# Hybrid encoder block on one core: softmax weights, q and k transposed by VectorE in 32x32 blocks and device memory instead of by TensorE

## The chip, the cores and the metric

The kernel runs on one core of a Trainium2 chip. The metric is the device time of one execution in microseconds (us). A core has TensorE (PE: matmuls out of SBUF into PSUM), VectorE (DVE), ScalarE (ACT), GpSimd (POOL) and SyncE (SP). Each works through its own list of instructions in order, and waits at an instruction until what that one needs is there. SP and POOL issue most DMA transfers here. The order of each list is fixed when the program is built.

## The reference

One layer on 512 tokens of width 1024, all float32: a half-step SwiGLU, a mixer, a second half-step SwiGLU. The mixer has a gated linear recurrence and a neighbourhood attention side by side. The part that matters here is the attention:

```python
h = _rmsnorm(x, norm_mix[l])
xr, gr, q, k, v, ga, gb = jnp.split(h @ w_in[l], splits, axis=-1)
...
q = _rmsnorm(q.reshape(B_, S, N_HEADS, HEAD_DIM), q_norm[l]) * (HEAD_DIM ** -0.5)
k = _rmsnorm(k.reshape(B_, S, N_HEADS, HEAD_DIM), k_norm[l])
y_att = _neighbourhood_attention(q, k, v, rel_pos_bias[l])   # 16 heads of 64, softmax over an 8x16 window
y = jax.nn.sigmoid(ga) * y_lru + jax.nn.sigmoid(gb) * y_att
x = x + y @ w_out[l]
```

## The kernel before

**Matmuls and chunks.** A float32 product is made of three fast passes: each operand is split into a high part (ACT copies it to the fast format, `wh`, `xh`) and a low part (DVE subtracts, `wl`, `xl`), and PE does high x high, low x high and high x low (`mm3`, L171 to L174). The weights of the middle stage come in blocks of 512 KB; SP loads a block into `wraw` (three buffers), ACT and DVE split it into `wh` and `wl` (four buffers each), and PE does 24 matmuls of 512 columns on it. Such a block with its 24 matmuls is called a chunk below.

**The order of chunks.** After the eight chunks of the recurrence input (`wxr`) come 24 chunks for q, k and v: heads 0 to 7 (the first half, `hf` 0) get four chunks for q, four for k, four for v, and then heads 8 to 15 (the second half) the same. Then come 24 gate chunks, eight for the GeLU gate, eight for gate A, eight for gate B (L1083 to L1103), and then eight output chunks (`wout`, L1110). Gate B chunk f is multiplied with the attention output `att[f]`, split into `yh`, `yl` and used as k-block f of every output chunk. So the loop over gate B asks for `att[f]` before it goes on: `until("att", ...)` at L1096, with the batches of `GB_BATCH` (f = 0 to 3, then 4 and 5, then 6, then 7).

**Attention is woven in between.** `heads(hf, raws, st)` is a generator. `weave` (L577) calls it a fraction of a step at each chunk (`RATE`: 0.75 steps in stage `t1`, 0.7 steps twice a chunk in stage `g`), and each `yield` ends a step. Both halves stand in one lane, the second behind the first. When `until` finds that `att[f]` isn't there, it runs all the steps that are missing, with no chunk between them.

**One half of the attention.** q and k come out of PE with tokens on the partitions (four tiles of 128 tokens each, `raws`). They are scaled by their norm (L902). `start(fi)` turns one pair of heads: eight PE transposes into PSUM (L911, L913), and from there ACT and DVE write the high and low parts (`qh`, `ql`, `kh`, `kl`). `scores` does the score matmuls (L943), then DVE adds the bias and takes the maximum (L963), ACT the exponential (L970), and DVE scales by the sum (L972, L975). The softmax weights of one block pair `n2` are in two tiles, `inner` (four 128x128 blocks) and `outer` (three). `turn` transposes those seven on PE (L982, L989) and ACT copies them out of PSUM. `apply` multiplies with V (L1006) and ACT writes `att`. A unit of this loop is one `n2` of one head pair in the first half (eight units), and a whole head pair in the second (four units).

**POOL's list.** POOL issues the copies that put the gates of the recurrence on other partitions (L759), the rearrangement of V through device memory (`vd` written at L860, read at L863 and L873), and the bias tiles `bm` (L885).

Of the kernel before, what the change touches and what calls it, by code (L numbers as in the profile page):

```python
# [9 lines left out]
F32 = mybir.dt.float32  # L10
F32R = mybir.dt.float32r
AF = mybir.ActivationFunctionType
ALU = mybir.AluOpType
# [3 lines left out]
P = 128  # L17
# [9 lines left out]
NCB, QC = 4, 16  # L27
# [64 lines left out]
def block_kernel(ctx: ExitStack, tc, a, out):  # L92
# [30 lines left out]
    def aux_t():  # L123
        return aux.tile([P, T], F32, tag="aux", name=nm("aux"))
# [126 lines left out]
    def hold(i):  # L251

        after(i, mark["mm"])
        return i
# [426 lines left out]
    gk = small[:, C_KN : C_KN + 1]  # L681

    state = {}

    def perm(ap):

        return ap.rearrange("p (r j c) -> p j r c", r=ROWS, j=NCB)
# [200 lines left out]

    def heads(hf, raws, st):

        rq = tiny.tile([P, 2, NCB, 8], F32, tag="rq", name=nm("rq"))
        for w in range(2):
            for j in range(NCB):
# [5 lines left out]
        for w in range(2):  # L899
            for j in range(NCB):  # L900
                t = raws[w][j].rearrange("p (h d) -> p h d", d=HD)
                hold(nc.vector.tensor_tensor(t, t, rq[:, w, j, :].unsqueeze(2).to_broadcast([P, 8, HD]), ALU.mult))  # L902
            yield
        qk, rss, soft, PTs = {}, {}, {}, {}


        def start(fi):
            fs = slice(fi * P, (fi + 1) * P)
            pq, pk = aux_t(), aux_t()
            for j in range(NCB):  # L910
                hold(nc.tensor.transpose(pq[:, j * P : (j + 1) * P], raws[0][j][:, fs], ident))  # L911
            for j in range(NCB):
                hold(nc.tensor.transpose(perm(pk)[:, j], raws[1][j][:, fs], ident))  # L913
            rev = lambda t: t.rearrange("p (j t) -> p j t", j=NCB)[:, :, ::-1]
            fwd = lambda t: t.rearrange("p (j t) -> p j t", j=NCB)
            qh, ql, kh, kl = (big_t(F32R, n=n) for n in ("qh", "ql", "kh", "kl"))
            nc.scalar.activation(rev(qh), fwd(pq), AF.Copy, scale=gq8)
            with tc.high_priority():
                nc.vector.scalar_tensor_tensor(rev(ql), fwd(pq), gq8, rev(qh.bitcast(F32)), ALU.mult, ALU.subtract)
            nc.scalar.activation(kh, pk, AF.Copy, scale=gk)  # L920
            with tc.high_priority():
                mark["kl"] = nc.vector.scalar_tensor_tensor(kl, pk, gk, kh.bitcast(F32), ALU.mult, ALU.subtract)
            grid = lambda t: t.rearrange("p (r c) -> p r c", r=ROWS)
            qk[fi] = qh, ql, grid(kh), grid(kl)

        def scores(fi, n2s):

# [47 lines left out]
                    nc.vector.tensor_scalar(pt, pt, rs[:, hp, n : n + 1], None, ALU.mult)  # L975
            return mm

        def turn(fi, n2):
            outer, inner = soft.pop((fi, n2))
            pT = aux_t()  # L980
            for q in range(4):
                hold(nc.tensor.transpose(pT[:, q * P : (q + 1) * P], inner[:, q * P : (q + 1) * P], ident))  # L982
            PTi = big_t(n="PT")
            with tc.high_priority():
                nc.scalar.activation(PTi, pT, AF.Copy)

            pT = aux_t()
            for q in range(3):
                hold(nc.tensor.transpose(pT[:, q * P : (q + 1) * P], outer[:, q * P : (q + 1) * P], ident))  # L989
            PTe = big_t(n="PT")  # L990
            with tc.high_priority():
                nc.scalar.activation(PTe[:, : 3 * P], pT[:, : 3 * P], AF.Copy)
            PTs[fi, n2] = PTe, PTi

        def apply(fi, behind=None):
            pv = aux_t()
            for n in range(NCB):
                PTe, PTi = PTs[fi, n // 2]
                for half in range(2):
                    if n in EDGE:  # L1000
                        vt = V[hf, "single" if half else "own", n]
                    else:
                        vt = V[hf, (KSTART[n] + half * QC) // 8]
                    for h2 in range(2):
                        q = (1 if half else h2 * 2) if n in EDGE else h2 * 2 + half
                        mm = nc.tensor.matmul(  # L1006
                            pv[h2 * HD : (h2 + 1) * HD, n * P : (n + 1) * P],
                            vt[:, (fi * 2 + h2) * HD : (fi * 2 + h2 + 1) * HD],
                            (PTe if n in EDGE else PTi)[:, q * P : (q + 1) * P],
                            start=half == 0, stop=half == 1)  # L1010
# [16 lines left out]
        def turns(i, k=0):  # L1027

            if not 0 <= i - LB < len(units):
                return False  # L1030
            fi, n2s = units[i - LB]
            turn(fi, n2s[k])
            return k + 1 < len(n2s)

        for i in range(len(units) + LC):
            together = phase[0] != "g"
            if together:
                turns(i)
            if i < len(units):
                fi, n2s = units[i]  # L1040
                last = scores(fi, n2s)
                if i >= LC and 1 in units[i - LC][1]:
                    apply(units[i - LC][0], last)
# [5 lines left out]
            if not together:  # L1049
                yield  # L1050
                if turns(i):
                    yield
                    turns(i, 1)
            if len(units) <= i < len(units) + LC and 1 in units[i - LC][1]:
                apply(units[i - LC][0])
            yield

    att = [None] * KT
    phase = ["t0"]
# [153 lines left out]
```

## Time and profile before

The median of three runs is 1116.77 us. The profiled execution spans 1114.8 us from its first to its last instruction.

| what | value |
|---|---|
| median of 3 runs | 1116.77 us (1116.19 to 1116.80) |
| profiled execution, span | 1114.8 us |
| idle time ahead of PE's groups | 1.1 us, all before the first matmul |
| DMA over the span | 161.16 MB, 145 GB/s |
| POOL queue / SP queue share of the DMA engines | 19.0% / 32.9% |

How to read the views: the page's first part has the busy time of each engine, its second the span in 40 slices, its fourth the chain of work that ended last. The groups of instructions give the line, the engine, the operation, output and inputs, the count, the busy time of the group, the mean duration of one in ns, and the idle time ahead of them. The timeline gives start and length of instructions in order of time, with equal neighbours merged (xN).

### The profile page before, as it was taken

To read this page: it belongs to the slowest core of one execution; us is meant where nothing else is said; L and a number is where in the kernel's file an instruction comes from. 1 tells how busy PE (TensorE), PEld (TensorE's weight loads), DVE (VectorE), ACT (ScalarE), POOL (GpSimd) and SP (SyncE) were. 2 spreads that over 40 slices of the span, in tenths; PEclk is the share of its full clock that TensorE was granted. 3 is DMA by queue.
4 is the path that set the end of the run, shared out by engine and by line. 5 is a ranking of instruction groups with operands and counts; after the bars stand their busy time and mean duration, and the time that the engine had idled before them with its cause. 6 is when DMAs were issued, how large, how long until landed. Compare 5 with 4: busy or idle time off the path is not lost.

```text
span 1114.8 us, 17726 instructions
## 1 busy us (share of the span) xinstructions
PE 1110.2 (100%) x6923; PEld 985.2 (88%) x6923; DVE 797.4 (72%) x1263; ACT 592.2 (53%) x903; POOL 109.8 (10%) x187
## 2 busy tenths in 40 slices
PE   9999999999999999999999999999999999999998
PEld 8899999988888778788888888888999999998887
DVE  7877777794745776999665976659877777784542
ACT  8554554563533678877364554346645444563330
POOL 0000000000000351250140000001000000000000
PEclk9999999999999999999999999999999999999999
DMA  8566656743423585673453332277766666652421
GB/s 266 154 168 152 156 154 164 166 137 95 137 84 111 165 249 153 178 195 100 137 162 100 99 100 74 77 246 156 198 148 163 153 168 145 160 170 96 132 76 38
DMA packets 54116, 161.16 MB, mean 145 GB/s; under 512 B 8464, under 2 KB 12048, under 8 KB 54032
## 3 DMA queue, kind: packets, MB, share of 16 engines
q1 hardware_dynamic: 39744, 118.31, 32.9%
q0 software_dynamic: 13712, 41.46, 19.0%
q8 instruction: 54, 0.88, 0.3%
q10 hardware_dynamic: 576, 0.26, 0.1%
q14 instruction: 30, 0.25, 0.1%
HBM read 143.19 MB, written 8.39 MB: 136 GB/s over the span
## 4 chain that ended last, share of the span: by engine, by line
PE 100%; DVE 0%; issue 0%
PE acc L312 31%; PE acc L172 11%; PE acc L173 10%; PE acc L174 10%; PE aux L312 5%; PE acc L831 4%; PE acc L832 4%; PE acc L833 4%; PE aux L172 4%; PE aux L173 4%; PE aux L174 4%; PE aux L1006 1%; PE aux L742 1%; PE aux L943 1%; PE aux L982 1%; PE acc L464 1%
## 5 line engine op out<-in xcount | busy, mean ns | idle before, releaser
L145 ACT ACTIVATE wh<-wraw 128x1024 fp32r<-128x1024 f32 (+3 forms) x224 | 220.7, 988 | 318.8 <-issue 93.4
L148 DVE TENSOR_TENSOR wl<-wraw,wh 128x1024 fp32r<-128x1024 f32 (+3 forms) x236 | 267.4, 1137 | 123.7 <-ACT wh L145 122.5
L312 PE MATMUL acc<-s,wh 128*128 128x256 f32 x1280 | 232.3, 283 | 0.0
L312 PEld LDWEIGHTS acc<-s,wh 128*128 128x128 f32 x1280 | 199.6, 192 | 0.1
L312 PE MATMUL acc<-s,wl 128*128 128x256 f32 x640 | 181.1, 283 | 0.0
L312 PEld LDWEIGHTS acc<-s,wl 128*128 128x128 f32 x640 | 122.9, 192 | 0.0
L172 PE MATMUL acc<-xh,wh 128*128 128x512 f32 x272 | 108.4, 398 | 0.0
L174 PE MATMUL acc<-xh,wl 128*128 128x512 f32 x272 | 106.6, 392 | 0.0
L173 PE MATMUL acc<-xl,wh 128*128 128x512 f32 x272 | 106.3, 391 | 0.0
L312 PE MATMUL acc<-xh,wl 128*128 128x256 f32 x320 | 90.6, 283 | 0.0
L312 PE MATMUL acc<-xl,wh 128*128 128x256 f32 x320 | 90.6, 283 | 0.0
L312 PE MATMUL acc<-xh,wh 128*128 128x256 f32 x320 | 90.5, 283 | 0.0
L831 PE MATMUL acc<-wh,xh 128*128 128x512 f32 x192 | 75.7, 394 | 0.0
L832 PE MATMUL acc<-wh,xl 128*128 128x512 f32 x192 | 74.8, 389 | 0.0
L833 PE MATMUL acc<-wl,xh 128*128 128x512 f32 x192 | 74.7, 389 | 0.0
L172 PE MATMUL aux<-hh,wh 128*128 128x512 f32 (+1 forms) x181 | 69.9, 386 | 0.0
L173 PE MATMUL aux<-hl,wh 128*128 128x512 f32 (+1 forms) x181 | 69.9, 386 | 0.0
L174 PE MATMUL aux<-hh,wl 128*128 128x512 f32 (+1 forms) x181 | 69.9, 386 | 0.0
L174 PE MATMUL acc<-hh,wl 128*128 128x512 f32 (+1 forms) x176 | 67.9, 386 | 0.0
L173 PE MATMUL acc<-hl,wh 128*128 128x512 f32 (+1 forms) x176 | 67.9, 386 | 0.0
L172 PE MATMUL acc<-hh,wh 128*128 128x512 f32 (+1 forms) x176 | 67.9, 386 | 0.0
L148 DVE TENSOR_TENSOR wl<-pair,wh 128x1024 fp32r<-128x1024 f32 x40 | 48.9, 1222 | 20.9 <-ACT wh L145 20.9
(225 smaller groups left out, 2288.9 us busy)
## 6 DMA issues: line engine op xcount, KB each, us to landing
wraw<-wqkv SPq DMA_DIRECT2D x24, 512.0 KB, 5.0
wraw<-wg SPq DMA_DIRECT2D x24, 512.0 KB, 3.6
wraw<-w1d SPq DMA_DIRECT2D x22, 512.0 KB, 3.6
wraw<-w2s SPq DMA_DIRECT2D x22, 512.0 KB, 4.1
pair<-w2s SPq DMA_DIRECT2D x22, 512.0 KB, 5.2
wraw<-w2d SPq DMA_DIRECT2D x22, 512.0 KB, 3.7
wraw<-w1s SPq DMA_DIRECT2D x18, 512.0 KB, 4.1
pair<-w1s SPq DMA_DIRECT2D x18, 512.0 KB, 5.5
```

The source lines that it names most:

```text
L145: nc.scalar.activation(H, raw, AF.Copy)
L148: return nc.vector.tensor_tensor(L, raw, H.bitcast(F32), ALU.subtract)
L172: nc.tensor.matmul(ps, wh, xh, start=first, stop=False, skip_group_check=skip)
L173: nc.tensor.matmul(ps, wh, xl, start=False, stop=False, skip_group_check=skip)
L174: mark["mm"] = nc.tensor.matmul(ps, wl, xh, start=False, stop=last, skip_group_check=skip)
L312: mm = nc.tensor.matmul(o, w_[:, c], x_, start=first and m + k == 0 and w_ is H and x_ is xh_, stop=m + k == 4 and w_ is L, skip_group_che ...
L464: nc.tensor.matmul(pre[i], w[i][1][:, s], xh[k], start=k == 0, stop=False)
L742: prev, mm = mm, nc.tensor.matmul(ps[d][b], W[w][o, c], X[x][o], start=x == 1, stop=w + x == 0)
L831: nc.tensor.matmul(pss[j], xh[kk][:, tj], H[:, s], start=kk == 0, stop=False)
L832: nc.tensor.matmul(pss[j], xl[kk][:, tj], H[:, s], start=False, stop=False)
L833: mark["mm"] = nc.tensor.matmul(pss[j], xh[kk][:, tj], L[:, s], start=False, stop=kk == KT - 1)
L943: mm = hold(nc.tensor.matmul(ps[hp][:, cs], q_[o, n * P : (n + 1) * P], keys(k_[o]), start=k_ is kl, stop=q_ is ql))
```

## The change

Nothing is transposed by PE in the attention any more. DVE has a transpose of 32x32 blocks; the blocks are then put in their places by a write to device memory and a read back.

- q and k: behind each scaling of a token tile, DVE transposes its blocks into `qkt`, and POOL writes it to `qd` in four DMAs: 8 tiles, 32 DMAs for each half. `fetch(g)` reads two head pairs of q and k back on SP, 512 KB each, into `xqk` (two buffers). `start` then reads `xqk` in place of PSUM. The norm weights of k are folded into q's.
- softmax weights: `ship` replaces `turn`. DVE transposes the blocks of `outer` and `inner` into `pt` (one buffer), POOL writes `pt` to `pd` (one DMA), and reads it back into `PT` (three buffers) in four DMAs, once for each unit and `n2`: 16 times.
- the steps: two more `yield`s and `fetch(0)` before the first `start`; in stage `g` each turn of the loop has three steps in both halves, and `ATT_LAG` is one number. `NBIG` goes from 48 to 43.

```diff
-ATT_LAG = (1, 2), (1, 2)
+ATT_LAG = 2, 2
...
-    NBIG = 48
+    NBIG = 43
...
                 hold(nc.vector.tensor_tensor(t, t, rq[:, w, j, :].unsqueeze(2).to_broadcast([P, 8, HD]), ALU.mult))
+                t2 = big_t(n="qkt")
+                nc.vector.transpose(
+                    t2.rearrange("p (c f i) -> p f c i", c=NCB, i=32), raws[w][j].rearrange("p (f c i) -> p f c i", c=NCB, i=32))
+                for ab in range(NCB):
+                    nc.gpsimd.dma_start(
+                        qd[w].rearrange("(c i) j a x -> j a i c x", c=NCB)[j, ab],
+                        t2[ab * 32 : (ab + 1) * 32].rearrange("p (c x) -> p c x", c=NCB))
             yield
+
+        def fetch(g):
+            for w in range(2):
+                x = big.tile([P, 16, 2, 32], F32, tag="xqk", bufs=2, name=nm("xqk"))
+                nc.sync.dma_start(
+                    x.rearrange("p x f i -> p x (f i)"), qd[w].rearrange("p j a (g x) -> g p (j a) x", g=2)[g])
+                for f in range(2):
+                    xs[w, g * 2 + f] = x[:, :, f]
+
+        yield
+        fetch(0)
+        yield
...
         def start(fi):
-            for j in range(NCB):
-                hold(nc.tensor.transpose(pq[:, j * P : (j + 1) * P], raws[0][j][:, fs], ident))
-            for j in range(NCB):
-                hold(nc.tensor.transpose(perm(pk)[:, j], raws[1][j][:, fs], ident))
...
+            if fi == 1:
+                fetch(1)
...
-        def turn(fi, n2):
+        def ship(fi, n2):
+
             outer, inner = soft.pop((fi, n2))
...
+            t = big.tile([P, NCB, 7, 32], F32, tag="pt", bufs=1, name=nm("pt"))
...
+            nc.vector.transpose(to[:, 4:], sub(outer, 3))
+            nc.vector.transpose(to[:, :4], sub(inner, 4))
+            d = dram.tile([P, NCB, 7 * 32], F32, tag="pd", bufs=4, name=nm("pd"))
+            nc.gpsimd.dma_start(d, t.rearrange("p c q i -> p c (q i)"))
+            PT = big.tile([P, NCB, 7, 32], F32, tag="PT", bufs=3, name=nm("PT"))
+            for j in range(4):
+                q = slice(j * 32, (j + 1) * 32)
+                nc.gpsimd.dma_start(PT[:, j].rearrange("p q i -> p (q i)"), d[q].rearrange("i c x -> c i x"))
...
-        LB, LC = ATT_LAG[hf]
+        LC = ATT_LAG[hf]
...
         for i in range(len(units) + LC):
...
+                behind = scores(fi, n2s)
+            if i >= LC and 1 in units[i - LC][1]:
+                apply(units[i - LC][0], behind)
+            if i < len(units):
+                for n2 in n2s:
+                    ship(fi, n2)
...
+            yield
+            if phase[0] == "g":
                 yield
-                if turns(i):
-                    yield
-                    turns(i, 1)
...
+                yield
```

The rows below are from the lists of the built programs: line, operation, output<-inputs, shape. The line numbers are each program's own; in the changed one the scores stand at L962, `apply` at L1024, the `qd` writes at L909, `fetch` at L917, the `pd` write and `PT` reads at L1006 and L1010.

PE before, at the first unit of the second half (the last two score matmuls, then the transposes for the next head pair, then a gate A chunk; the eleventh of the 24 gate chunks stands ahead of the score matmuls):

```order
L943 MATMUL acc_6391<-kh_6368,ql_6367 128x256
L943 MATMUL acc_6390<-kh_6368,ql_6367 128x256
L911 MATMUL aux_6456<-ident,qk_5090 128x128
L911 MATMUL aux_6456<-ident,qk_5092 128x128
L911 MATMUL aux_6456<-ident,qk_5094 128x128
L911 MATMUL aux_6456<-ident,qk_5096 128x128
L913 MATMUL aux_6457<-ident,qk_5323 128x8x16
L913 MATMUL aux_6457<-ident,qk_5325 128x8x16
L913 MATMUL aux_6457<-ident,qk_5327 128x8x16
L913 MATMUL aux_6457<-ident,qk_5329 128x8x16
L172 MATMUL acc_6478<-xh_3088,wh_6480 128x512
```

PE after, at the same first unit of the second half, which now stands behind the chunk of gate B f=5, the 22nd of the 24:

```order
L172 MATMUL acc_6789<-xh_3102,wh_6791 128x512
L173 MATMUL acc_6789<-xl_3103,wh_6791 128x512
L174 MATMUL acc_6789<-xh_3102,wl_6792 128x512
L962 MATMUL aux_6810<-kl_6784,qh_6781 128x256
L962 MATMUL aux_6809<-kl_6784,qh_6781 128x256
L962 MATMUL aux_6810<-kh_6783,qh_6781 128x256
```

And PE after, from the end of that unit's 24 score matmuls to the next unit's:

```order
L962 MATMUL acc_6812<-kh_6783,ql_6782 128x256
L962 MATMUL acc_6811<-kh_6783,ql_6782 128x256
L962 MATMUL aux_6929<-kl_6900,qh_6897 128x256
L962 MATMUL aux_6928<-kl_6900,qh_6897 128x256
L962 MATMUL aux_6929<-kh_6899,qh_6897 128x256
```

The second half's scores moved behind 22 gate chunks, where eleven stood ahead of them before, and there is no chunk between the first and the second unit. From there PE's list reads: scores of units 0, 1 and 2, `apply` of unit 0, scores of unit 3, `apply` of unit 1, the chunk of gate B f=6, half of `apply` of unit 2, 14 matmuls of the chunk of f=7, the other half of unit 2, the rest of f=7 and 13 matmuls of output chunk 0, half of `apply` of unit 3, 19 more matmuls of output chunks 0 and 1, and the other half of unit 3.

POOL before, where V of the second half is rearranged in the stage of the first half's attention (`vd` is the device memory copy, `va` and `ve` the edge tiles):

```order
L863 DMA vs_5666<-vd_82 128x1x512
L869 MEMSET ve_5669 128x512
L873 DMA va_5668<-vd_82 64x4x64 x2
L873 DMA ve_5669<-vd_82 64x4x64
L873 DMA va_5668<-vd_82 64x4x64 x2
L873 DMA ve_5669<-vd_82 64x4x64
L869 MEMSET ve_5678 128x512
L873 DMA va_5677<-vd_82 64x4x64 x2
L873 DMA ve_5678<-vd_82 64x4x64
L873 DMA va_5677<-vd_82 64x4x64 x2
L873 DMA ve_5678<-vd_82 64x4x64
L885 DMA bm_5942<-rpb 128x640
```

POOL after, from the end of that same rearrangement:

```order
L873 DMA va_5587<-vd_82 64x4x64 x2
L873 DMA ve_5588<-vd_82 64x4x64
L885 DMA bm_5651<-rpb 128x640
L885 DMA bm_5930<-rpb 128x640
L885 DMA bm_5932<-rpb 128x640
L1006 DMA pd_5634<-pt_5631 128x896
L1010 DMA PT_5636<-pd_5634 128x1x224 x4
L1006 DMA pd_5794<-pt_5791 128x896
L1010 DMA PT_5796<-pd_5794 128x1x224 x4
```

The round trips of the first half's units 2 and 3 stand behind the rearrangement of V; before, nothing of the attention but bias tiles stood behind it.

POOL after, at the second half (the last two of the eight groups of q and k writes, and the first round trips):

```order
L909 DMA qd_6573<-qkt_6673 32x4x128 x4
L909 DMA qd_6573<-qkt_6680 32x4x128 x4
L885 DMA bm_7024<-rpb 128x640
L885 DMA bm_7026<-rpb 128x640
L1006 DMA pd_6880<-pt_6877 128x896
L1010 DMA PT_6882<-pd_6880 128x1x224 x4
L885 DMA bm_7144<-rpb 128x640
L1006 DMA pd_6890<-pt_6887 128x896
L885 DMA bm_7146<-rpb 128x640
L1010 DMA PT_6892<-pd_6890 128x1x224 x4
L1006 DMA pd_6999<-pt_6996 128x896
L1010 DMA PT_7001<-pd_6999 128x1x224 x4
```

The four reads of each round trip stand right behind its write, and the next write behind them; eight such groups follow each other for the second half. Before, POOL had only the bias tiles there.

More of the change, by code (lines that the diff above doesn't have):

```diff
@@ L680, in block_kernel @@
     nc.vector.tensor_scalar(gq8, small[:, C_QN : C_QN + 1], HD**-0.5, None, ALU.mult)
-    gk = small[:, C_KN : C_KN + 1]
+    nc.vector.tensor_tensor(gq8, gq8, small[:, C_KN : C_KN + 1], ALU.mult)
     state = {}
@@ L889, in heads @@
     def heads(hf, raws, st):
+        xs = {}
+        qd = [dram.tile([P, NCB, NCB, P], F32, tag="qd", bufs=4, name=nm("qd")) for _ in range(2)]
         rq = tiny.tile([P, 2, NCB, 8], F32, tag="rq", name=nm("rq"))
@@ L909, in start @@
[L909 to L915 removed]
+            xq, xk = (xs[w, fi].rearrange("p (j a) i -> p j a i", j=NCB) for w in range(2))
@@ L997, in apply @@
             for n in range(NCB):
-                PTe, PTi = PTs[fi, n // 2]
+                PT = PTs[fi, n // 2]
                 for half in range(2):
@@ L1024, in heads @@
         yield
-        LB, LC = ATT_LAG[hf]
[L1027 to L1033, printed above, removed]
+        LC = ATT_LAG[hf]
         for i in range(len(units) + LC):
-            together = phase[0] != "g"
-            if together:
-                turns(i)
+            behind = None
             if i < len(units):
                 fi, n2s = units[i]
-                last = scores(fi, n2s)
-                if i >= LC and 1 in units[i - LC][1]:
-                    apply(units[i - LC][0], last)
+                behind = scores(fi, n2s)
[4 more added lines that the diff above has]
+                    ship(fi, n2)
                 if 0 in n2s:
```

36 lines of the change are left out of this document (12 added, 24 removed).

## The prediction

> **What bounds the kernel now.** First the page's busy times, then the span in slices, then the chain.
>
> ```profile
> span 1114.8 us, 17726 instructions
> PE 1110.2 (100%) x6923; PEld 985.2 (88%) x6923; DVE 797.4 (72%) x1263; ACT 592.2 (53%) x903; POOL 109.8 (10%) x187
> PE   9999999999999999999999999999999999999998
> PE 100%; DVE 0%; issue 0%
> ```
>
> PE is busy in every slice, and the chain that ended last is PE alone. So PE's list is the time: what leaves it counts in full, and so does each new wait in it. No other engine matters until it makes PE wait. The span and the median of 1116.77 us lie 2.0 us apart; I work against the span and add the 2.0 at the end.
>
> **What is removed.** Here are transposes among matmuls in PE's timeline (start, length), then the two groups of the softmax weights and the two of q and k.
>
> ```profile
> 651.75 0.39 PE L174 MATMUL acc<-xh,wl 128*128 128x512 f32 x1
> 651.98 0.60 PE L982 MATMUL aux<-ident,p 128*128 128x128 f32 x4
> 652.41 0.49 PE L989 MATMUL aux<-ident,p 128*128 128x128 f32 x3
> 652.66 0.48 PE L172 MATMUL acc<-xh,wh 128*128 128x512 f32 x1
> 652.98 0.40 PE L173 MATMUL acc<-xl,wh 128*128 128x512 f32 x1
> L982 PE MATMUL aux<-ident,p 128*128 128x128 f32 x64 | 9.6, 272 | 0.0
> L989 PE MATMUL aux<-ident,p 128*128 128x128 f32 x48 | 7.9, 273 | 0.0
> L911 PE MATMUL aux<-ident,qk 128*128 128x128 f32 x32 | 5.1, 281 | 0.0
> L913 PE MATMUL aux<-ident,qk 128*128 128x128 f32 x32 | 5.0, 273 | 0.0
> ```
>
> The groups' busy sums make 27.6, but neighbours overlap. Without the seven transposes L172 and L173 would start 0.23 and 0.46 after 651.75, at 651.98 and 652.21; L173 starts at 652.98, so seven cost 0.77, or 0.11 each. 64 + 48 + 32 + 32 = 176 of them by 0.11 give **R = -19.4**. All transposes of the attention are gone from PE's new list.
>
> **What the order does to the second half.** Its scores now stand behind 22 gate chunks, 11 later than before, and hardly any work is left to PE while eight softmax round trips run. This is the largest term. Prices: a chunk by PE's pitch, then a unit of the second half (scores, `apply`, and the DVE operation that ends its softmax and the next head's `kl`).
>
> ```profile
> 654.12 0.39 PE L172 MATMUL acc<-xh,wh 128*128 128x512 f32 x1
> 655.25 0.39 PE L174 MATMUL acc<-xh,wl 128*128 128x512 f32 x1
> 655.57 0.39 PE L943 MATMUL aux<-kl,qh 64*128 64x256 f32 x2
> 657.25 0.44 PE L1006 MATMUL aux<-PT,va 128*64 128x128 f32 x4
> 659.14 0.66 PE L911 MATMUL aux<-ident,qk 128*128 128x128 f32 x4
> 662.86 0.74 DVE L922 SCALAR_TENSOR_TENSOR kl<-aux,small,kh 128x512 fp32r<-128x512 f32 x1
> ```
>
> Five matmuls in 1.13 are 0.227 each, so a chunk of 24 is 5.4. Scores take 657.25 - 655.57 = 1.7, `apply` 1.9, and a unit on DVE from the first score to the end of `kl` 663.60 - 655.57 = 8.0.
>
> For POOL: the times of an issue, and of a write to device memory until the read that waits for it (the `vd` rows are the only round trip of this sort in the trace, the bracket has the wait).
>
> ```profile
> 476.23 0.60 POOL L860 DMA_DIRECT2D vd<-v  x1 [0.65 <-DVE v L856]
> 477.48 0.60 POOL L860 DMA_DIRECT2D vd<-v  x1 [0.66 <-DVE v L856]
> 481.85 0.59 POOL L863 DMA_DIRECT2D vs<-vd  x1 [0.78 <-DMA vd<-v]
> 484.97 0.59 POOL L863 DMA_DIRECT2D vs<-vd  x1 [2.52 <-DMA vd<-v]
> 552.72 0.91 POOL L860 DMA_DIRECT2D vd<-v  x1 [0.62 <-DVE v L856]
> 557.23 0.60 POOL L863 DMA_DIRECT2D vs<-vd  x1 [3.59 <-DMA vd<-v]
> L885 POOL DMA_DIRECT2D bm<-rpb x16 | 8.8, 552 | 111.2 <-DVE rs L972 54.0 <-DVE nmx L963 52.4 <-DMA gate<-pair 4.0
> L873 POOL DMA_DIRECT2D va<-vd x16 | 12.4, 776 | 9.5 <-issue 9.3
> bm<-rpb POOLq DMA_DIRECT2D x16, 320.0 KB, 4.2
> xd<-pair SPq DMA_DIRECT2D x16, 256.0 KB, 2.6
> va<-vd POOLq DMA_DIRECT2D x16, 64.0 KB, 3.5
> wraw<-wqkv SPq DMA_DIRECT2D x24, 512.0 KB, 5.0
> 494.99 3.69 DVE L902 TENSOR_TENSOR qk<-qk,rq 128x512 f32<-128x512 f32 x6
> ```
>
> From write to read 481.85 - 476.23 = 5.6 and 484.97 - 477.48 = 7.5. The `vd` write of 552.72 is the last of its kind and its reader starts 4.5 later. I take 5.2 for `pd`, between 4.5 and 5.6; 7.5 is the high end, and the low one 3.2, by SP's writes to device memory, which land in 2.6 behind an issue of 0.6. An issue is 0.55 for 128 rows (`bm`) and 0.78 for 256 (`va`): 0.55 for `pd` and `PT`, 0.65 for the smaller pieces of `qd`.
>
> The reads stand behind the wait for their own write, and the next write behind them. So a ship holds POOL for 5.2 + 4 x 0.55 = **7.4**, and nothing overlaps with the next one.
>
> Set t = 0 where PE ends gate B f=3. Until t = 10.9 PE has the chunks f=4 and f=5. DVE's list puts the eight q and k transposes from behind gate B f=1's product (ready at t = -10.9, then a weight split and two scalings) to just ahead of f=4's (t = 5.4): the first at about -6.6, the last at 5.7.
> - POOL: 32 `qd` writes by 0.65 from -6.6 end at 14.2; the last lands 3.5 later, 17.7; SP's fetch in 256-byte pieces, 5.0 by the `wqkv` row, 22.7; ACT and DVE split, 2 x 0.75 with handoffs, and the scores of the first unit start at **24.7**. PE has waited since 10.9.
> - The first `pt` is ready 8.0 + 1.2 (its two transposes) after: 34. Eight ships by 7.4 are 59, two bias issues stand between, and POOL is through at 94.3. The last read lands after 4 (between 4.2 and 3.5): 98.3. `apply` of that half, the copy, two DVE operations and the split of `y` take 4 more: 102.3, and only then can PE go on with the output chunks.
> - In that time PE has the chunks of gate B f=4 and f=5, four scores, four `apply`, the chunks f=6 and f=7, and 44 matmuls of the first output chunks that need no `att[7]` (32 ahead of the last half of `apply`, 12 behind it): 10.9 + 6.8 + 7.6 + 10.9 + 44 x 0.227 = 46.2.
>
> So **C = 102.3 - 46.2 = +56**. With 5.4 for a ship (3.2 + 2.2) it is 40, and with 9.7 (7.5 + 2.2) it is 74; the `qd` issues at 0.55 take 3 off and at 0.78 add 4, and dear transposes (below) add 5: 37 to 83.
>
> The cost of DVE's block transpose is in no row. The cheap end is an operation on half the elements, 0.42; the nearest row, L902 above on the same elements, makes six in 3.69, 0.6 each, which I take. A recurrence on the same shape is the dear end, 1.2.
>
> ```profile
> L963 DVE CUSTOM_DVE_ANT_0 so<-aux,bm 128x256 f32<-128x256 f32 x24 | 10.1, 419 | 0.0
> L784 DVE TENSOR_TENSOR_SCAN th<-gate,gate 128x512 f32<-128x512 f32 x4 | 4.9, 1216 | 0.0
> ```
>
> At 1.2 the last `qkt` and the first unit are later by about 5 in sum, at 0.42 earlier by 1. The Trainium skill, "VectorE: DVE Perf Modes", section "The three transpose paths", gives 311 ns for 128x128 in bf16 and, under "Rules for kernel authors", advises TensorE for 128x128 where PSUM can take the result; it speaks against this change. By its figure an estimate for 128x512 is 1.24 us, near the dear end, and the sum would be 1173. No run before shows the operation.
>
> **The first half.** Its units are woven between chunks, so that PE waits only for what is late.
>
> ```profile
> 508.51 0.40 PE L833 MATMUL acc<-wl,xh 128*128 128x512 f32 x1
> 501.22 0.78 POOL L873 DMA_DIRECT2D ve<-vd  x1
> 563.83 0.54 POOL L869 MEMSET ve<- 128x512 f32 x1
> 578.49 0.77 POOL L873 DMA_DIRECT2D ve<-vd  x1 [0.24 <-issue]
> ```
>
> Before, the q and k transposes follow 508.51; now `yield`s put four chunks there, so the first scores are asked for at 508.7 + 21.8 = 530.5. POOL is free of V's first rearrangement at 502.0; 32 writes by 0.65 end at 522.8, landing 526.3, fetch 531.3, split 533: **A = +3** (0 where the issues take 0.55, 9 with issues of 0.78 and a landing of 5).
>
> Its ships meet V's second rearrangement on POOL, whose edge tiles alone run from 563.83 to 579.26. Counted through PE's new list from 533 by the prices above, PE wants the weights of units 0 and 1 at 561 (24 scores a unit pair, two chunks and a half between) and those of units 2 and 3 at 585. POOL's list has the first two ships ahead of the edge tiles and the next two behind them. Before 563.83 POOL stood waiting for V's landings, so that I let unit 1's weights land at 565, 4 late. Units 2 and 3 follow at 579.3: 579.3 + 2 x 7.4 + 4 = 598 stands against 585 + 4, 9 late, of which I take 8 since PE's earlier waits count only once: **B = 4 + 8 = +12**, from 0 (ships of 5.4 and two chunks more of cover) to 18 (ships of 9.7).
>
> Hidden: ACT's copies of PSUM go (ACT idles half its time), the folded norm weight, `NBIG` and one bias tile earlier or later. SP waits at `fetch` with weight loads behind it, but its loads run some seven chunks ahead (three raw and four split buffers), and that covers a wait of up to 20 (four chunks).
>
> **Sum:** -19.4 + 3 + 12 + 56 = +51.6; 1114.8 + 51.6 + 2.0 = **1168**.
>
> **Rivals.**
> 1. *Faster: the ships are short enough to be covered*, and R alone is left: 1116.8 - 19.4 = 1097. The point from which it turns: even with A = B = 0, C has to be under 19.4, so that eight ships take 37 less than 59, 2.8 each, when their four reads alone take 2.2 to issue and the shortest write in a row above needs 3.2. For it: only that the trace of before has no ship. Chance 0.03, and 0.02 that it ends within 0.2%.
> 2. *DVE is the bound and not POOL*, since two ships fit into a unit: 4.6 each. Then DVE's 8.0 + 1.2 a unit sets the pace: 24.7 + 4 x 9.2 + 7.4 + 8 = 77, C = 31, the time 1143. Against it: a ship of 4.6 leaves 2.4 from write to read, under the 3.2 of the low end. For it: the rows of `vd` queue behind other writes, which `pd` doesn't. Chance 0.12.
> 3. *PE runs slower after its waits.* In the first row of matmuls after PE's only idle time
>
> ```profile
> L138 PE MATMUL aux<-ones 128*128 128x128 f32 x16 | 3.8, 431 | 1.1 <-DVE pol L667 1.1
> ```
>
>    16 of 128x128 took 3.8, 0.24 each against 0.11 for those above. If each long wait of the drain (14 ahead of the first unit, then about six of 5 to 10) costs that once more, half of 2 to 4 us of work each time is lost, +8: 1176. The Trainium skill, "TensorE: Matmul & The Clock Gate", section "HAM oscillation — how this bites in real kernels", states that rule: after some 3.4 us idle the clock halves until PE has been busy for a while. That row agrees for the start; no row shows it within the kernel. Chance 0.23.
> 4. *The edit isn't what it says*, and transposes stay on PE: PE's list excludes it, under 0.01.
>
> **How the numbers follow.** The forecast's own case has 0.59: 1168, with its own range of 1152 to 1186 by the ends of a ship. Rival 2 (0.12) gives 1143 and rival 3 (0.23) 1176. The lowest sum of all low ends is 1114.8 - 19.4 + 0 + 0 + 37 + 2 = 1134, the highest 1114.8 - 19.4 + 9 + 18 + 83 + 2 + 8 = 1215; not all ends come together, so the range of 8 in 10 runs from 1140 to 1200. A measurement here tells 0.2%, or 2.2 us, from no change. Faster 0.03, same 0.02, slower 0.95.
>
> **What will show it.** Right: PE's idle time 60 to 80 us in one place late in the mixer, with POOL's `PT` and `pd` issues 7.4 apart eight times over, releaser the landing of `pd`; the first scores of the second half wait about 14 for `kh`; PE's busy sum falls by 27.6 while the gaps grow; the chain names POOL and DMA. Wrong in R: a neighbour pitch other than 0.227 where transposes went. Wrong in C: ship periods far from 7.4, or PE working in the gaps. Wrong in A or B: waits ahead of L962 or `apply` in the first half other than 3 and 12. The clock rival: matmul pitches near 0.45, or a granted clock under 1.00, behind gaps.

## The result and the profile after

| | before | after |
|---|---|---|
| median | 1116.78 us (1116.19 to 1117.07) | 1211.65 us (1208.93 to 1212.47) |
| span of the profiled execution | 1114.8 us | 1209.7 us |
| mean granted TensorE clock over the span | 1.000 | 0.953 |

The change made the kernel slower: ratio 1.0845 (95% interval 1.083 to 1.0861), 94.9 us. The sign was forecast; the predicted 1168 lies 43 us under the measured time, and the range ended at 1200.

The page of the changed kernel: span, busy times, the slices of PE and of its granted clock (the share of TensorE's full clock that it was given, in tenths), and the chain.

```profile
span 1209.7 us, 17700 instructions
PE 1112.6 (92%) x6747; PEld 983.2 (81%) x6747; DVE 823.9 (68%) x1312; ACT 582.4 (48%) x874; POOL 197.6 (16%) x331
PE   9999999999999999897869962468999999999998
PEclk9999999999999999899879985588999999999999
PE 32%; issue 1%; DMA 0%; POOL 0%; DVE 0%
```

PE has gaps in two places, slices 17 to 21 (the first half's attention) and 24 to 28 (the second half's), and in the same slices the granted clock falls. PE's busy time has not fallen by the 27.6 of the removed groups: it grew by 2.4. The chain could be followed back only to the last `pd`, 33% of the span in sum, so the sign that it would name POOL and DMA is not decided by it.

What PE waited for (total, times, longest):

```profile
PE aux L1024 <- DMA PT<-pd: 58.4, 10, 11.6
PE aux L962 <- DVE kl L939: 27.9, 4, 11.1
PE acc L831 <- ACT qk L843: 4.9, 1, 4.9
PE aux L1024 <- issue: 1.3, 1, 1.3
```

That is 92.5 of new waits. The bill, all from the two profiled executions: +92.5 of waits; -18.5 for the 176 transposes (the sum of their start-to-start times in the trace of before); and the rest to 94.9 is +20.9, which is time in which the same matmuls ran slower. By place, 27.7 of the waits lie in the first half's stage (4.9 + 11.6 + 0.6 + 10.6) and 64.8 behind gate B f=5.

POOL's timeline through two ships of the second half (start, length, idle time ahead and what ended it):

```profile
745.70 0.58 POOL L1006 DMA_DIRECT2D pd<-pt  x1
746.25 0.56 POOL L885 DMA_DIRECT2D bm<-rpb  x1
751.31 2.04 POOL L1010 DMA_DIRECT2D PT<-pd  x3 [4.50 <-DMA pd<-pt]
755.58 0.66 POOL L1010 DMA_DIRECT2D PT<-pd  x1 [2.23 <-issue]
756.23 0.60 POOL L1006 DMA_DIRECT2D pd<-pt  x1
761.67 2.00 POOL L1010 DMA_DIRECT2D PT<-pd  x3 [4.85 <-issue]
765.96 0.66 POOL L1010 DMA_DIRECT2D PT<-pd  x1 [2.28 <-issue]
766.61 0.60 POOL L1006 DMA_DIRECT2D pd<-pt  x1
```

From one `pd` to the next 756.23 - 745.70 = 10.5, and then 10.4, against 7.4 in the prediction. From write to read it is 5.6 and 5.4, against 5.2 assumed (in the eight ships of the second half 4.9 to 7.3, 5.8 in the mean). The four reads take 4.9 in place of 2.2: 0.67 each, and the fourth doesn't follow the third at once but stands still for 2.2 first. In all eight ships of the second half it starts 0.32 to 0.36 after the landing of the first read (755.22 for the one of 755.58, 765.63 for 765.96). From the first `pd` at 733.71 to the end of the last read's issue at 820.2 the eight ships take 86.5, so 10.8 each.

PE behind a long wait, in the first half:

```profile
580.03 1.12 PE L1024 MATMUL aux<-PT,vs 128*64 128x128 f32 x8 [11.62 <-DMA PT<-pd]
581.93 0.80 PE L172 MATMUL acc<-xh,wh 128*128 128x512 f32 x1
582.53 0.63 PE L173 MATMUL acc<-xl,wh 128*128 128x512 f32 x1
582.96 0.63 PE L174 MATMUL acc<-xh,wl 128*128 128x512 f32 x1
583.38 0.43 PE L172 MATMUL acc<-xh,wh 128*128 128x512 f32 x1
583.65 0.40 PE L173 MATMUL acc<-xl,wh 128*128 128x512 f32 x1
583.88 0.39 PE L174 MATMUL acc<-xh,wl 128*128 128x512 f32 x1
```

The pitch is the time from the start of one matmul to the start of the next. After 11.6 us of standing still, L173 starts 0.60 behind L172, the next one 0.43 behind it, and from 583.65 the pitch is 0.23 again: some 3.5 us of work at about half pace. This is the third rival, which I had left out of the sum.

### The profile page after: what moved, and what is told of

Its sections match the earlier page's. It is cut to its first block, busy times and chain, and to the rows that moved or that the text cites. A ratio compares the mean times of both kernels' runs of the same rounds, so it can differ in the third digit from the quotient of the medians.

```text
span 1209.7 us, 17700 instructions
## 1 busy us (share of the span) xinstructions
PE 1112.6 (92%) x6747; PEld 983.2 (81%) x6747; DVE 823.9 (68%) x1312; ACT 582.4 (48%) x874; POOL 197.6 (16%) x331
## 5 line engine op out<-in xcount | busy, mean ns | idle before, releaser
L172 PE MATMUL acc<-xh,wh 128*128 128x512 f32 x272 | 109.6, 403 | 0.0
L173 PE MATMUL acc<-xl,wh 128*128 128x512 f32 x272 | 108.1, 397 | 0.0
L831 PE MATMUL acc<-wh,xh 128*128 128x512 f32 x192 | 76.5, 399 | 4.9 <-ACT qk L843 4.9
L148 DVE TENSOR_TENSOR hl<-h,hh 128x512 fp32r<-128x512 f32 x88 | 57.2, 687 | 21.8 <-PE aux L173 21.5
L172 PE MATMUL aux<-hh,wh 128*128 128x512 f32 (+1 forms) x181 | 69.9, 386 | 0.0
L173 PE MATMUL aux<-hl,wh 128*128 128x512 f32 (+1 forms) x181 | 69.9, 386 | 0.0
L173 PE MATMUL acc<-hl,wh 128*128 128x512 f32 (+1 forms) x176 | 67.9, 386 | 0.0
L172 PE MATMUL acc<-hh,wh 128*128 128x512 f32 (+1 forms) x176 | 67.9, 386 | 0.0
```

What stands on the lines that cost most here:

```text
L148: return nc.vector.tensor_tensor(L, raw, H.bitcast(F32), ALU.subtract)
L172: nc.tensor.matmul(ps, wh, xh, start=first, stop=False, skip_group_check=skip)
L173: nc.tensor.matmul(ps, wh, xl, start=False, stop=False, skip_group_check=skip)
L831: nc.tensor.matmul(pss[j], xh[kk][:, tj], H[:, s], start=kk == 0, stop=False)
```

## Experiments

The time of the kernel before on the same chip stands in brackets. A time without a range is that of a single run, and the changed kernel's own runs lie up to 3.5 us apart, so that less than that between two such runs says nothing. These theories were to be told apart first: that the **ships** (a softmax round trip on POOL: one `pd`, four `PT`) make the loss, that the **late order** of the second half does, and that the trip of q and k does.

### Reads on SP, and one read on SP

```diff
-                nc.gpsimd.dma_start(PT[:, j].rearrange("p q i -> p (q i)"), d[q].rearrange("i c x -> c i x"))
+                nc.sync.dma_start(PT[:, j].rearrange("p q i -> p (q i)"), d[q].rearrange("i c x -> c i x"))
```

> The four PT reads of each ship are issued by SP, nothing else is changed. Theory (the chain of ships on POOL sets the drain, 10.8 us each, of which 4.9 are the reads): POOL's part of a ship is the pd issue alone, the next one waits for pt, that is for the landing of pd (about 5) and two block transposes (1.2): a period of about 6.7 in place of 10.8, so 8 x 4 = 32 us less wait in the second half, some 10 less in the first, and some 5 less at the low clock: about 1165 (1150 to 1185). Rival (the landing of the reads and DVE's blocked softmax set the drain, not POOL's list): within 8 us of 1211. Rival (SP's waits hold the weight loads): PE waits for wh or wl in the gate chunks, and the time does not fall.

Measured 1186.03 (before: 1116.15), span 1184.3. POOL's timeline then has nothing but the writes:

```profile
738.86 0.55 POOL L1006 DMA_DIRECT2D pd<-pt  x1 [7.21 <-DVE nmx L982]
747.34 0.55 POOL L1006 DMA_DIRECT2D pd<-pt  x1 [7.93 <-DVE pt L1004]
755.42 0.54 POOL L1006 DMA_DIRECT2D pd<-pt  x1 [7.53 <-DVE pair L1104]
763.39 0.54 POOL L1006 DMA_DIRECT2D pd<-pt  x1 [7.43 <-DVE pt L1004]
```

The period is 8.2 in place of 10.8, not the 6.7 expected: `pd` now lands 6.4 after its issue (4.9 before), and the one `pt` is free only then. So the time falls by 25.6, a little less than the range had. PE waited neither for `wh` nor for `wl`, so SP's waits didn't hold the weight loads.

The next kernel moves only the fourth read (`nc.sync if j == 3 else nc.gpsimd`).

> Only the fourth PT read of each ship goes to SP. Theory (the fourth read is held until the first has landed, 2.3 us, and costs 0.66 to issue): a ship is 7.8 on POOL in place of 10.8, 8 x 3 = 24 less in the second half and about 5 in the first: about 1183 (1172 to 1195). Rival (the hold belongs to whatever comes fourth on POOL's queue behind a landing): the next pd write is held in its place and the period stays near 10: 1205 or more.

Measured 1191.14 (before: 1116.15), within the expected range. POOL:

```profile
752.48 0.61 POOL L1006 DMA_DIRECT2D pd<-pt  x1
758.45 1.99 POOL L1010 DMA_DIRECT2D PT<-pd  x3 [5.36 <-PE acc L962]
760.43 0.59 POOL L1006 DMA_DIRECT2D pd<-pt  x1
765.91 2.06 POOL L1010 DMA_DIRECT2D PT<-pd  x3 [4.88 <-issue]
767.96 0.59 POOL L1006 DMA_DIRECT2D pd<-pt  x1
```

The next `pd` follows three reads without a hold, and a ship is 7.5 to 8.0. So it is a fourth read that is held, not whatever stands fourth, and taking that hold and its issue off POOL was worth 20 us.

### One kind of transpose undone

q and k by PE again, the rest as changed (`start` as before, no `qkt`, `qd` and `fetch`, `NBIG` 47):

```diff
-            xq, xk = (xs[w, fi].rearrange("p (j a) i -> p j a i", j=NCB) for w in range(2))
+            for j in range(NCB):
+                hold(nc.tensor.transpose(pq[:, j * P : (j + 1) * P], raws[0][j][:, fs], ident))
+            for j in range(NCB):
+                hold(nc.tensor.transpose(perm(pk)[:, j], raws[1][j][:, fs], ident))
```

> q and k are transposed by PE again, in the changed kernel's order; the softmax weights go through device memory as in the changed kernel. Theory: the ships stay at 10.8 and end as much earlier as the first scores of the second half need no round trip (11 us of wait for kl go), 64 transposes by 0.105 come back (+6.7), the late ACT copy ahead of the q and k chunks (4.9) may go: 1198 to 1208. Rival (the q and k trip and its DMAs are the main loss): under 1170.

Measured 1190.49 (before: 1116.15): 8 less than the range, so more of the loss hung on the q and k trip than I had allowed. The waits fell from 92.5 to 62.5: those for `kl` from 27.9 to 11.4, the 4.9 ahead of L831 is gone, and so are 6 of the first half's for `PT`. Of the 62.5, 16.5 lie in the first half and 46.0 in the second.

The other way round: the kernel before, with q and k through device memory and the softmax weights by PE in the order of before, but for two more steps ahead of each half's first unit, with which the second half's scores stand behind 16 gate chunks (11 before, 22 in the changed kernel).

> q and k go through device memory as in the changed kernel; the softmax weights are transposed by PE again, with the order of steps of the kernel before (so the second half starts earlier than in the changed kernel). Theory (the ships of the softmax weights in the late second half are the loss): 64 transposes less, 6.7, and at most 5 us of new waits, so 1108 to 1118. Rival (the q and k trip makes the first scores late whatever the order): over 1125, with waits ahead of the first L962 of the second half.

Measured 1131.81 (before: 1116.15). The rival was right:

```profile
PE aux L962 <- DVE kl L939: 13.0, 1, 13.0
PE acc L831 <- ACT qk L843: 4.9, 1, 4.9
```

So 64 transposes less bring 6.7 by the price of 0.105 each, the trip costs 17.9 of waits, and the rest to 15.7, some 4.5, is slower matmuls. Against before, q and k alone cost 15.7 and the softmax weights alone 74.3; together they cost 94.9.

### The order alone

```diff
+        for _ in range(15 * hf):
+            yield
         qk, rss, soft, PTs = {}, {}, {}, {}
```

> The kernel before, with all transposes on PE, and 15 more steps ahead of the second half's first unit, so that its scores stand behind 21 gate chunks in place of 11. Theory: lateness costs by itself what four units of about 9 us on DVE and ACT leave uncovered by PE's remaining work, 15 to 35 us: 1131 to 1151, so that of the second half's 65 us of waits in the changed kernel less than half is the order and the rest the round trips. Rival (the order is nearly all of it): over 1165. Rival (PE's transposes need no cover): within 5 of 1116.

Measured 1126.41 (before: 1116.6), less than expected: moving the second half behind 21 gate chunks costs 10 us while PE does the transposes, 7.2 of it waits. The order is not the loss by itself. Whether it makes the ships dear, because PE's other work is gone when they run, is what the next kernel tries: softmax weights through device memory, with an earlier second half.

> As e3_qk_pe (q and k by PE, softmax weights through device memory), but with two steps a turn in the first half's gate stage and none extra ahead of the first unit, so that the second half's scores stand some eight steps (31 us) earlier. Theory (the end is set by 16 ships in a row on POOL, 10.8 each, with V's rearrangement between them): waits and half-pace matmuls move from the second half to the first, the ships close up, and the time falls from 1190 by 20 to 40: 1150 to 1170. Rival (ships cost what they cost wherever they stand, since PE waits for each): 1180 or more. Rival (lateness was the loss): under 1130.

```diff
-        yield
-        yield
         qk, rss, soft, PTs = {}, {}, {}, {}
...
             if phase[0] == "g":
-                yield
-                yield
+                for _ in range(1 + hf):
+                    yield
```

Measured 1186.41 (before: 1116.58), only 4 less than with the late second half, hardly more than runs of one kernel differ; the rival was right, and 57.6 of waits are left. The first `pd` of the second half goes out at 687.89 in place of 716.47, but eight ships still take 90 us, and PE has 48 gate matmuls (10.9), a unit's scores and an `apply` (3.6) to each two ships, which take 22. The waits moved more than they went: the second half's fell from 46.0 to 24.5, since its units now have chunks between them, and the first half's, with a step less in each turn, rose from 16.5 to 33.1. As I read it, PE's other work is the only cover there is, and the ships of the two halves together need more of it than there is. Lateness by itself was 10 of the 74, and an earlier start gives back less than that.

### One row of ships, or overlapping ones

q and k by PE as in the second pair of runs, reads on SP, and two buffers for `pt`:

```diff
-            t = big.tile([P, NCB, 7, 32], F32, tag="pt", bufs=1, name=nm("pt"))
+            t = big.tile([P, NCB, 7, 32], F32, tag="pt", bufs=2, name=nm("pt"))
```

> As e3_qk_pe (q and k by PE, late second half), but the PT reads are issued by SP and pt has two buffers (45 in the shared ring in place of 47), so that a ship no longer holds POOL nor DVE until it has landed. Theory (the ships cost because they stand in one row, each holding POOL and the one pt until it is through): two ships of a unit overlap, DVE's 9.2 a unit sets the pace in place of 21, and the time falls from 1190 to 1140 to 1160. Rival (the latency of a trip, 10 us from the write to the last landing, is paid by PE for each apply whatever overlaps): 1170 or more, with waits of 5 to 10 ahead of each apply.

Measured 1154.82 (before: 1116.34), as expected. POOL's `pd` writes of the second half:

```profile
702.11 0.55 POOL L991 DMA_DIRECT2D pd<-pt  x1 [3.50 <-DVE pt L989]
703.16 0.55 POOL L991 DMA_DIRECT2D pd<-pt  x1 [0.51 <-DVE nmx L967]
710.82 0.55 POOL L991 DMA_DIRECT2D pd<-pt  x1 [3.23 <-DVE pt L989]
711.86 0.55 POOL L991 DMA_DIRECT2D pd<-pt  x1 [0.49 <-DVE nmx L967]
725.96 0.54 POOL L991 DMA_DIRECT2D pd<-pt  x1 [13.55 <-DVE pt L989]
729.01 0.54 POOL L991 DMA_DIRECT2D pd<-pt  x1 [2.51 <-DVE pt L988]
```

The two writes of a unit go out 1.05 apart in the first two units (3 and 6.5 apart in the last two), though each still lands 3 to 7 later. From the first `pd` to the last are 41.9 us, where one row took 71.0 (716.47 to 787.47). With the same trips, and the same late order, 36 of the 74 are gone: they were the price of a single row, not of the latency. (How much of it the second `pt` brought was not tried by itself; the reads on SP alone had brought 25.6 in the changed kernel.) What is left in the second half are waits of 2 to 6 for `kl` and ahead of `apply`, 29.8 in sum.

### The clock

Extra matmuls, whose result the real ones overwrite, fill the waits of the changed kernel, up to 90 of 128x256 ahead of the second half of an `apply` and up to 44 of 128x512 ahead of a unit's scores:

```diff
+                if n == 2:
+                    for _ in range(FILL[hf, fi]):
+                        hold(nc.tensor.matmul(pv[:, 2 * P :], xh[0][:, :P], xh[0][:, : 2 * P], start=True, stop=True))
```

> The changed kernel with extra matmuls (their result is overwritten) ahead of the instructions that wait longest, as many as fill about the wait; nothing else waits on them. Theory (the matmuls run at half pace for some us behind each wait, 21 us in sum): the granted clock stays near 1.00, the pitch of 0.43 goes, and the time falls by 12 to 20: 1191 to 1200. Rival (the slow pitch comes from something else than PE standing still, or costs nothing since the ships set the end): 1207 or more.

Measured 1221.45 (before: 1116.6): slower, though the mean clock rose to 0.985 and the time lost to slow matmuls between the second half's first scores and its last `apply` fell from 13 us to about 4. The last wait for `PT` ends at 825.85 against 823.41, but the first scores had started 3.1 later too (727.75 against 724.61): that stretch took 98.1 in place of 98.8. Where ships set the end, faster matmuls only wait longer. The other 7.4 lie behind it: with the extra matmuls the 32 output matmuls (7.3) that stood ahead of the last `apply` now stand behind it.

So I filled only the two long waits of the first half.

> The changed kernel with extra matmuls only ahead of the two long waits of the first half (84 and 78 of 128x256, about as long as the waits). Theory (behind each long wait PE runs at half pace for about 4 us of work, which costs in full here, since no ship is late there): the matmuls behind 580 and 619 run at 0.23 and the time falls by 3 to 6, to 1206 to 1209. Rival (slow pitch costs nothing there either, as in e7_warm, where the ships set the end): 1211 to 1213. If the extra matmuls overshoot the waits, more than 1213.

Measured 1209.0 (1202.75 to 1210.17), ratio 1.0816 (1.0794 to 1.0839), against 1.0845 (1.083 to 1.0861): the intervals overlap, and the time alone settles nothing. The pitch does:

```profile
578.41 0.66 PE L1033 MATMUL aux<-PT,vs 128*64 128x128 f32 x8 [0.82 <-DMA PT<-pd]
579.43 0.50 PE L175 MATMUL acc<-xh,wh 128*128 128x512 f32 x1
579.76 0.40 PE L176 MATMUL acc<-xl,wh 128*128 128x512 f32 x1
580.00 0.40 PE L177 MATMUL acc<-xh,wl 128*128 128x512 f32 x1
```

At the same place the matmuls now start 0.33 and then 0.24 apart, where it was 0.60 and then 0.43, and the eight of `vs` take 0.66 in place of 1.12. Standing still is what halves the pace. (The trace is that of the fastest of the four runs, 1202.75.)

### A version that beats both

From the run with q and k through memory: the second half's scaling, writes and first fetch are pulled into the first half's loop, and the five buffers that were free are used.

```diff
+            if hf == 0 and phase[0] == "g" and 4 <= i < 9:
+                next(lanes["att"][1])
             yield
```

> As e4_p_pe (q and k through device memory, softmax weights by PE), but the second half's scaling, writes and first fetch are pulled into the turns of the first half's loop, three steps ahead, and the buffers that the softmax round trip had taken are given back (49 in place of 44). Theory (e4's loss of 15.7 is the 13.0 of late first scores, the 4.9 of ACT's late copy, which lacks a buffer, and the low clock behind both): both waits go and the 64 transposes less are left: 1109 to 1112. Rival (the late copy has another cause than buffers): 1114 to 1117 with a wait of 5 ahead of the q and k chunks. Rival (the trip can't be hidden): over 1120.

Measured 1117.06 against 1116.6, ratio 1.0003 (0.9993 to 1.0013). The 13.0 is gone; the 4.9 is left, so more buffers were not what ACT's copy lacked. ACT's list shows why it is late: the four copies of q (L843) stand behind a table load and four operations of the recurrence (L777).

```profile
498.83 1.28 ACT L777 ACT_TABLE_LOAD   x1
500.13 2.19 ACT L777 ACTIVATE th<-th 128x512 f32<-128x512 f32 x4
502.22 2.04 ACT L843 ACTIVATE qk<-acc 128x512 f32<-128x512 f32 x4
```

In the kernel before, the copies run from 495.40 on, ahead of that table load (500.62). As I read it, the `qkt` tiles take turns in the shared ring of buffers, and each turn shifts which older tile a copy has to wait for, and so its place in the list; that step isn't shown. With a ring of their own (and 46 in the shared one):

```diff
-                t2 = big_t(n="qkt")
+                t2 = big.tile([P, T], F32, tag="qkt", bufs=4, name=nm("qkt"))
```

> As e5_p_pe_early, but the transposed tiles qkt have four buffers of their own, so that the shared ring of buffers is used in the same turn as in the kernel before; ACT's list then has the copies of the second half's q ahead of the recurrence's square roots again. Theory (e5 came out even because 4.9 of wait and some 2.5 of slow matmuls behind it ate the 6.7 of the 64 transposes): both go, 1108.5 to 1111. Rival (the scores or something else in PE's list got slower by itself): 1114 to 1117 without that wait.

Measured 1109.45 (1109.36 to 1110.03) against 1116.58: ratio 0.9938 (0.9924 to 0.9952). The page:

```profile
span 1107.6 us, 17738 instructions
PE 1102.7 (100%) x6859; PEld 978.1 (88%) x6859; DVE 805.0 (73%) x1280; ACT 597.0 (54%) x905; POOL 145.7 (13%) x251
PE   9999999999999999999999999999999999999998
```

PE has no gap again, ACT's first copies of q are back ahead of the table load (495.36), and 7.1 us are won for 64 transposes, 0.11 each. (The ring of its own and the smaller shared ring were not tried apart.)

The same for everything, with `pd` and `PT` on SP, the second half's scaling, writes and fetch early and four steps a turn there, was tried too.

> The changed kernel with the pd writes and PT reads issued by SP, the second half's scaling, writes and fetch pulled into the first half's loop, two steps a turn of the loop in the first half's gate stage and four in the second, and a lag of one unit there, so that the last apply stands three chunks ahead of the output chunks. Theory (nothing in the round trips is dear for PE if they start early enough and don't queue on POOL): the waits fall under 15 in all and the 18.5 of the transposes are left: 1100 to 1115. Rival (SP's waits hold the weight loads, or ships are too slow to keep up with the units): 1120 to 1160, with waits ahead of apply or of the gate chunks.

Measured 1184.01 (before: 1116.6), ratio 1.0595 (1.0571 to 1.062): the rival's cause was right, ships too slow for the units, but the time lies 24 above its range. PE stands 57.6 ahead of `apply`, in eleven waits of 2 to 8. `pt` still has one buffer and SP the one row, so that ships are no closer: on SP `pd` goes out at 585.63, 594.67 and 605.27.

## Why the prediction was wrong

**R, -19.4.** Right: 18.5 by the trace, and 7.1 for 64 in the last version, where nothing else moved.

The bill by the terms, measured less predicted: waits of the first half 27.7 - 15 (A and B), waits of the second half 64.8 - 56 (C), slower matmuls 20.9 - 0, R 0.9: 12.7 + 8.8 + 20.9 + 0.9 = 43.3. This bill counts what PE did, not what made it late: 13 of the 20.9 lie between the second half's first scores and its last `apply`, where the ships set the end. Told by what set the end, the last `apply` came 22.5 later than C had it, the first half's waits were 12.7 more, R 0.9, and the 7.2 that are left are near the 7.9 of slower matmuls outside that stretch.

**C, +56, is the step that failed, in its size: the price of a ship.** The mechanism was as told: eight ships in one row on POOL, nothing overlapping, PE idle while they run. The scores started at t = 22.0 (24.7 predicted) and the first `pd` went out at 31.1 (34). But "5.2 + 4 x 0.55 = 7.4" was 10.8. The write to read was near: 5.8 in the mean. The reads were not: 4.9 in place of 2.2. I took 0.55 each from `bm`, whose issues stand alone or in pairs, and they were 0.67; and I let four reads of one ship follow each other. The fourth waits for the landing of the first. The rows of `va`, "9.5 <-issue 9.3", quoted and not read, had held issues of this kind: the one of 492.08 starts 0.33 behind the landing, at 491.75, of the one of 486.02. So the last `apply` could go on at t = 120.8 and not 98.3, 22.5 later. Of these, some 9 show as waits of PE; the rest is PE's own work there, which ran slower (56.0 us in place of 42.5 by my prices). That the ship was the price, and not something that came with it, the runs show: with the fourth read taken off POOL the period fell to 7.5 to 8.0 and the time by 20, and with two ships overlapping half of the loss of the softmax weights went.

Two readings behind the 5.2 were wrong, with little weight. The read of 557.23 starts before the `vd` write of 552.72 has landed (557.59), so that the 4.5 is no trip; it waited for the write of 551.47, 5.8 before. And the low end of 3.2 adds an issue of 0.6 to a landing of 2.6 that is already counted from the issue's start.

**B, +12, was 22.8**, for the same reason. The fourth read of unit 1 was held 3.9 (575.70) with V's edge tiles behind it, those ended at 590.5 and not 579.3, and units 2 and 3 went out behind them.

**A, +3**, had no wait at all ahead of the first scores, but ACT's copy of the second half's q, a step that I counted at nothing with the buffers, came 4.9 late. The runs with q and k through memory show on what it hung, the place of these copies in ACT's list: with more buffers it stayed, with a ring for `qkt` it went.

**The clock, rival 3 with a chance of 0.23 and +8**, was there in every run with long waits, and larger: 20.9 us of slower matmuls, for which the sum had nothing. By the pitch in the trace 13 of them lie among the second half's waits; there the run with all waits filled shows that they cost nothing by themselves, since the ships set the end. The rest, some 8, lies in the first half's stage (5) and behind the last `apply` (3). It followed from my own forecast of long waits and belonged into the sum.

**DVE's transposes** were no part of it:

```profile
L1004 DVE STREAM_TRANSPOSE pt<-p 128x512 f32<-128x512 f32 x16 | 11.0, 687 | 5.2 <-DMA pd<-pt 5.2
L906 DVE STREAM_TRANSPOSE qkt<-qk 128x512 f32<-128x512 f32 x16 | 10.7, 693 | 0.0
L1003 DVE STREAM_TRANSPOSE pt<-p 128x384 f32<-128x384 f32 x16 | 9.0, 564 | 25.0 <-DMA pd<-pt 25.0
```

0.69 for 128x512 is near the 0.6 taken from L902, and far from the estimate of 1.24 worked out from the Trainium skill ("VectorE: DVE Perf Modes", "The three transpose paths"): the measurement decides. The last column has what they do to others: 30.2 us in which DVE stood ahead of a transpose until the one `pt` had landed, with the next unit's maxima and `kl` behind it. What that costs PE stays open: the waits for `kl` fell from 27.9 to 11.4 with q and k on PE and one `pt`, and only to 10.8 with two, so that most of them belong to the q and k trip.

**The rivals.** That the time ends faster was possible for a part: with q and k alone, early enough and with buffers of their own, PE's list is shorter by 7.1 and nothing waits. I had looked for it in the length of a ship, where it doesn't lie. "DVE is the bound" came true nowhere: even with overlapping ships the first writes of the units stood 11.8 apart in the mean (702.11 to 737.52), not 9.2. Of the four only the third, the clock, came true, on top of the forecast's own case.

## What to carry to other kernels

Work that is moved from a full engine to a chain of DMAs is worth what the full engine saves only if the chain has its own row: price a round trip by all that stands in its queue's order, a read that is held until an earlier one has landed too, and compare the period, not the latency, with the work that covers one unit. Expect the pace of PE behind a long wait to be lower, and put it into the sum as soon as the sum has long waits. Where the same ring of buffers serves everything, a new tile in it can move waits to places that have nothing to do with it; here a ring of its own (with a smaller shared one) took the wait away.

## What the runs showed of the hardware

- A fourth read of 128 rows of 896 bytes, issued by POOL, starts 0.32 to 0.36 behind the landing of the first, while 64 KB writes of 512-byte pieces went out 28 in a row at 0.55 with four to eight not yet landed. What the limit is counted in was not tried.
- `pd` landed 4.9 after its issue (the median) in the changed kernel, and 6.4 with nothing but the reads moved to SP.
- Behind waits of 4 to 12 us PE's pitch was 0.43, until 3.4 to 5.9 us after the wait's end; behind waits of 1.3 and 1.4 us it was 0.34 once and then 0.23. Filling the wait took the slow pitch away (0.33, then 0.24). This agrees with the rule of the Trainium skill, "TensorE: Matmul & The Clock Gate", "HAM oscillation — how this bites in real kernels".
